# Opening of a hybrid decoder block on one core: small constants loaded behind the norm of x, large transfers first, identity transposes ahead of the first turns, TensorE too in written order

## The chip, the cores and the metric

One core of one Trainium2 chip runs the whole program. The metric is the device time of one launch in microseconds (us), lower is better. The core has TensorE (PE; its weight loads are the rows PEld), VectorE (DVE), ScalarE (ACT), GpSimd (POOL) and SyncE (SP, which here only issues DMAs; ACT issues some too).

## The reference

A decoder block on x of 1 x 1024 x 1024 in float32. What matters here is its beginning:

```
u = rms_norm(h, mix_pre_g)                        # x * rsqrt(mean(x*x) + eps) * g
z = einsum('bsd,de->bse', u, w_in)                # d = 1024, e = 512 + 3*512 + 2*1024
p, q, k, v = z[..., :o1], z[..., o1:o2], z[..., o2:o3], z[..., o3:o4]
lam = exp(sum(lam_q1*lam_k1)) - exp(sum(lam_q2*lam_k2)) + lambda_init
```

Then follow a pooling mixer (p, scaled by pool_scale), differential attention on four heads (q, k, v, lam, gain subln_g), two sigmoid gates, an output projection and a SwiGLU network of width 2816.

## The kernel before, in words

Every float32 matrix is split in two float32r parts, hi (a cast, on ACT) and lo = value - hi (a subtraction, on DVE or POOL), and a product is three matmuls: hi*hi, lo*hi, hi*lo (`mac`, L105 to L107; `triple`, L230 to L232).

The opening works on eight blocks of 128 tokens, `tb` 0 to 7. For each, SP loads 128 x 1024 of x (`load_x`, L302). ACT squares and sums it (`square`, L127), DVE makes the mean (`ms`, L122), POOL the power -0.5 (`rstd`, L123), DVE multiplies x by it and by the gain `g1` (`normed`, L348). PE turns the block with eight 128 x 128 transposes against an identity (`x_t`, L379; I call this a turn) into one of two PSUM buffers of the tag "pair". From there ACT casts `A_hi` (L383), DVE subtracts `A_lo` (L86), and ACT copies a plain float32 version (`A_raw` for blocks 0 to 3, L399; `S_raw` for 4 to 7, L402), from which DVE builds the sums S1 to S4 that the later units need (L159). Meanwhile the q and k weights of heads 0 and 1 come in as four tiles of 1024 x 128 (`w_raw`, L205), cast by ACT (`w_hi`, L327) and split by POOL (`w_lo`, L332, in four pieces).

As soon as two blocks are turned, `first_pair` multiplies them for head 0: q and k, 24 matmuls of 256 columns each (a half pair is one of the two). There are four pairs. Then come head 1's q and k, 4 times 24 matmuls of 512 columns (`common(1, ...)`), and then fourteen units of the projection. A unit (`seven`, L250 to L280) is seven products of 12 matmuls of 512 columns with operands A11, S1, S2, A12, S3, S4, A22 and weight sums made by `weights` (`Wh`, `Wl`, `wf_t`). Results of heads 0 to 3 go through `qk_done` (ACT L310 or L163, DVE L311 or L86, a store by ACT, L314) to DRAM.

The scheduler of the language sets the order on an engine, except inside `tc.manual_schedule` (L358), where the named engines keep the written order; before, these are ACT, DVE and POOL, and PE is left to the scheduler. Six small constants (`psc`, `sgc`, four lambda vectors into a tile `sg`; L430 to L434) are written behind the opening but no data holds them back, and the scheduler puts their DMAs first on ACT.

Every DMA of SP and ACT signals one of eight counters, and a DMA that takes up a counter again first waits for its earlier transfer.

Of the kernel before, what the change touches and what calls it, by code (L numbers as in the profile page):

```python
# [31 lines left out]
A8, B4 = 16, 14  # L32
QORDER = (7, 0, 6, 1, 5, 2, 4, 3)
LAG = 4
PACES = (2.2, 0.5, 0.3, 0.3)


@with_exitstack
def block_kernel(ctx, tc, x, w_in, pool_mix, pool_scale, w_branch_a, lam_q1, lam_k1, lam_q2,
# [42 lines left out]
    def f32(ap):  # L82
        return ap.bitcast(F32)
# [221 lines left out]
    def qk_done(h, e, t, src, st=None):  # L305
# [44 lines left out]
    for tb in range(2):  # L350
        xts.append(load_x(tb))
    nc.sync.dma_start(g1, mix_pre_g.partition_broadcast(P))
    xts.append(load_x(2))
    first_raw(0)
    first_raw(1)
    for tb in range(3, 5):
        xts.append(load_x(tb))
    with tc.manual_schedule(engines={nc.scalar.engine, nc.vector.engine, nc.gpsimd.engine}):  # L358
        for tb in range(2):
            square(tb)  # L360
            rstd(tb)
        for tb in range(2):
            normed(tb)
# [5 lines left out]
        o = [(fil("q"), fil("k")), (mm("q"), mm("k"))]

        def first_pair(i):
            for e in range(2):
                common(0, e, i // 2, o[i // 2][e], slice(i % 2 * 2 * P, (i % 2 + 1) * 2 * P))

        for tb in range(NB):
            t, cols = tb // 4, slice(tb % 4 * P, (tb % 4 + 1) * P)
            both = pair("x_t")
            for k in range(KD):
                nc.tensor.transpose(both[:, k // 4, k % 4 * P:(k % 4 + 1) * P], xts[tb][:, k * P:(k + 1) * P], ident)  # L379
            v = [both[:, kq, :].rearrange("p (k t) -> p k t", k=4) for kq in range(2)]  # L380
            ops = [[a[:, :, cols] for a in U[f"A{t + 1}{kq + 1}"]] for kq in range(2)]
            for kq in range(2):
                nc.scalar.copy(ops[kq][0], v[kq])  # L383
            if tb + 3 < NB:
                square(tb + 3)
            if tb in (0, 2, 4):
                first_hi(tb // 2 + 1)
            for kq in range(2):
                sub(ops[kq][1], v[kq], ops[kq][0])
            if tb + 2 < NB:  # L390
                normed(tb + 2)
            if tb + 3 < NB:
                rstd(tb + 3)
            if tb < 6:
                for part in range(2):
                    first_lo(tb // 2 + 1, part + tb % 2 * 2)
            if t == 0:
                for kq in range(2):
                    nc.scalar.copy(traws[f"A1{kq + 1}"][:, :, cols], v[kq])  # L399
            else:  # L400
                s1, s2, s3, s4 = (traws[f"S{i + 1}"][:, :, cols] for i in range(4))
                nc.scalar.copy(s1, v[0])  # L402
                tt(s1, v[1], s1, ALU.add)
                tt(s2, s1, s2, ALU.subtract)
                tt(s3, v[1], s2, ALU.subtract)
                tt(s4, s4, s2, ALU.subtract)
            if tb + 5 < NB:
                xts.append(load_x(tb + 5))
            if tb < 2:
                first_raw(tb + 2)  # L410
            if tb in (3, 5, 7):
                first_pair(tb // 2 - 1)
            if tb == 7:
                for e in range(2):
                    qk_done(0, e, 0, o[0][e])
    first_pair(3)
    for e in range(2):
        qk_done(0, e, 1, o[1][e])
    W = weights(w_cols(o_q, 2), w_cols(o_k, 2))
    for t in range(2):  # L420
        o = (fil("q"), fil("k")) if t == 0 else (mm("q"), mm("k"))
        for e in range(2):
            common(1, e, t, o[e], slice(0, HALF))
            qk_done(1, e, t, o[e])
    for n in ("S1", "S2", "S3", "S4"):
        U[n] = operand(n)
        split(U[n], traws[n])
# [4 lines left out]
    lamt = temp("sg").rearrange("p (i d) -> p i d", d=HD)
    for i, t in enumerate(lams):
        nc.scalar.dma_start(lamt[:, i, :], t.partition_broadcast(P))  # L434
    lsum, lexp, nlam = small(2, "lsum"), small(2, "lexp"), cp.tile([P, 1], F32, name="nlam")
    for i in range(2):
        nc.vector.tensor_tensor_reduce(out=lamt[:, 4, :], in0=lamt[:, 2 * i, :], in1=lamt[:, 2 * i + 1, :],
                                       scale=1.0, scalar=0.0, op0=ALU.mult, op1=ALU.add,
                                       accum_out=lsum[:, i:i + 1])
    nc.scalar.activation(lexp, lsum, AF.Exp)  # L440

    nc.vector.tensor_tensor(out=nlam, in0=lexp[:, 1:2], in1=lexp[:, 0:1], op=ALU.subtract)
    nc.vector.tensor_scalar(nlam, nlam, -LAMBDA_INIT, None, op0=ALU.add)
    nc.scalar.mul(sgc, sgc, 1.0 - LAMBDA_INIT)
    for g, w in enumerate(WINDOWS):
        nc.gpsimd.iota(cnt[:, g, :], pattern=[[1, 16]], base=1, channel_multiplier=0,
                       allow_small_or_imprecise_dtypes=True)
        nc.vector.tensor_scalar(cnt[:, g, :], cnt[:, g, :], float(w), None, op0=ALU.min)
# [692 lines left out]
```

## Time and profile before

| what | value |
|---|---|
| median of 3 runs | 1298.51 us (1295.7 to 1298.53) |
| the profiled execution, its own time | 1296.83 us |
| its span, first to last instruction | 1295.0 us |
| PE busy, of the span | 1250.5 us (97%) |
| DVE, ACT, POOL busy | 837.8, 581.2, 139.5 us |
| mean granted TensorE clock | 0.997 |

The profile shows the profiled execution alone; its own time is 1.83 us above its span, which lies around the first and last instruction. A busy PE is not PE at its peak, since matmuls overlap and their ends are modelled; the spacing of starts is the better measure of pace. PE is idle nearly only at the ends of the span: the first of forty slices is 40% busy, the second 80%, the last 70%, the others 90% or more apart from two at 80%.

### The profile page before, as it was taken

The page shows a single profiled execution, that of the slowest core. Times are in us where ns is not written, and L with a number is a line of the kernel's source. Part 1 is how long each engine was busy: PE and PEld are TensorE (multiplying, and loading weights), DVE is VectorE, ACT ScalarE, POOL GpSimd, SP SyncE. Part 2 cuts the span into 40 slices and gives each one's busy share as a digit, 9 for nine tenths or more (in the row PEclk, how much of TensorE's full clock was granted, in tenths as well). Part 3 has the DMA queues.
Part 4 walks back from the last instruction along what each step waited for, and adds up shares of the span by engine and source line. Part 5 has one row for each costly group of instructions (what it writes and reads, how often), then busy time and mean ns, then how long its engine had stood idle before and what let it go on. Part 6 is the DMA issues. An engine that isn't in the chain of part 4 may idle for free.

```text
span 1295.0 us, 15657 instructions
## 1 busy us (share of the span) xinstructions
PE 1250.5 (97%) x5856; PEld 1036.0 (80%) x5856; DVE 837.8 (65%) x1301; ACT 581.2 (45%) x1033; POOL 139.5 (11%) x128
## 2 busy tenths in 40 slices
PE   4899999999989998999999999999999999999997
PEld 4788778888778887878878888888888888888886
DVE  4875676444369997655499565565565538965666
ACT  6443335344486675144464333333333334444542
POOL 3100000000101010001102101111110111000221
PEclk9999999999999999999999999999999999999999
DMA  7254346332598411543333232333223258732235
GB/s 247 67 179 161 104 148 207 120 130 103 166 284 220 143 54 57 160 165 131 113 107 109 93 101 99 104 122 119 85 90 114 98 195 291 256 104 90 90 106 203
DMA packets 139788, 179.16 MB, mean 138 GB/s; under 512 B 8000, under 2 KB 94528, under 8 KB 137280
## 3 DMA queue, kind: packets, MB, share of 16 engines
q1 hardware_dynamic: 127776, 146.56, 35.7%
q10 hardware_dynamic: 11936, 31.60, 6.4%
q8 instruction: 46, 0.75, 0.2%
q14 instruction: 30, 0.25, 0.1%
HBM read 124.39 MB, written 53.74 MB: 138 GB/s over the span
## 4 chain that ended last, share of the span: by engine, by line
PE 81%; DVE 7%; DMA 4%; ACT 4%; issue 2%; POOL 1%; ACTq 0%; DVEq 0%; SPq 0%; POOLq 0%
PE Y L230 10%; PE Y L231 10%; PE Y L232 9%; PE X L230 5%; PE X L232 5%; PE X L231 5%; PE Yd L231 3%; PE Yd L232 3%; PE Yd L230 2%; PE Z L231 2%; PE Z L232 2%; PE Z L230 2%; PE o L653 2%; PE wo L794 2%; PE wo L795 2%
## 5 line engine op out<-in xcount | busy, mean ns | idle before, releaser
L159 DVE TENSOR_TENSOR p<-Z,p 128x512 f32<-128x512 f32 x35 | 24.2, 691 | 158.8 <-PE Z L232 158.8
L231 PE MATMUL Y<-A_lo,Wh 128*128 128x512 f32 x296 | 115.7, 391 | 0.3 <-DVE A_lo L86 0.3
L230 PE MATMUL Y<-A_hi,Wh 128*128 128x512 f32 x296 | 115.3, 390 | 0.0
L232 PE MATMUL Y<-A_hi,Wl 128*128 128x512 f32 x296 | 115.2, 389 | 0.0
L230 PE MATMUL X<-S_hi,Wh 128*128 128x512 f32 x280 | 109.1, 390 | 0.1
L231 PE MATMUL Y<-S_lo,Wh 128*128 128x512 f32 x280 | 109.2, 390 | 0.0
L230 PE MATMUL Y<-S_hi,Wh 128*128 128x512 f32 x280 | 109.1, 390 | 0.0
L232 PE MATMUL Y<-S_hi,Wl 128*128 128x512 f32 x280 | 109.1, 390 | 0.0
L232 PE MATMUL X<-S_hi,Wl 128*128 128x512 f32 x280 | 109.0, 389 | 0.0
L231 PE MATMUL X<-S_lo,Wh 128*128 128x512 f32 x280 | 109.0, 389 | 0.0
L199 ACT CAST Wh<-wf_t 128x1024 fp32r<-128x1024 f32 x70 | 72.6, 1050 | 70.3 <-PE X L231 30.8
L86 DVE TENSOR_TENSOR w_op<-wd,w_op 128x512 fp32r<-128x512 f32 x77 | 56.3, 731 | 53.6 <-ACT w_op L163 53.5
L86 DVE TENSOR_TENSOR Wl<-wf_t,Wh 128x1024 fp32r<-128x1024 f32 x70 | 86.6, 1245 | 4.7 <-ACT Wh L199 4.7
L199 ACT CAST Wh<-w_raw 128x1024 fp32r<-128x1024 f32 x72 | 60.4, 841 | 63.1 <-PE Z L231 41.9
L163 ACT CAST w_op<-wd 128x512 fp32r<-128x512 f32 x77 | 47.9, 622 | 80.7 <-PE Yd L232 32.5
L86 DVE TENSOR_TENSOR Wl<-w_raw,Wh 128x1024 fp32r<-128x1024 f32 x72 | 69.6, 967 | 14.4 <-ACT Wh L199 14.4
L231 PE MATMUL Yd<-w_op,s_op 128*128 128x512 f32 x176 | 68.7, 390 | 0.3 <-DVE w_op L86 0.2
L230 PE MATMUL Yd<-w_op,s_op 128*128 128x512 f32 x176 | 68.6, 390 | 0.0
L232 PE MATMUL Yd<-w_op,s_op 128*128 128x512 f32 x176 | 68.3, 389 | 0.0
L159 DVE TENSOR_TENSOR wf_t<-w_raw,wf_t 128x512 f32<-128x512 f32 x70 | 65.8, 940 | 1.0
L231 PEld LDWEIGHTS Y<-A_lo,Wh 128*128 128x128 f32 x296 | 55.6, 188 | 12.0 <-DVE A_lo L86 0.7
L230 PEld LDWEIGHTS Y<-A_hi,Wh 128*128 128x128 f32 x296 | 55.6, 188 | 11.5
(259 smaller groups left out, 3050.6 us busy)
## 6 DMA issues: line engine op xcount, KB each, us to landing
s_raw<-fsd SPq DMA_DIRECT2D x35, 512.0 KB, 3.5
w_raw<-in_w_in_dram SPq DMA_DIRECT2D x32, 512.0 KB, 3.9
w_raw<-in_w_ffn_gate_dram SPq DMA_DIRECT2D x22, 512.0 KB, 3.6
w_raw<-in_w_ffn_up_dram SPq DMA_DIRECT2D x22, 512.0 KB, 3.6
fsd<-fss SPq DMA_DIRECT2D x11, 1024.0 KB, 3.9
wd<-in_w_ffn_down_dram SPq DMA_DIRECT2D x44, 256.0 KB, 5.3
fsd<-F SPq DMA_DIRECT2D x33, 256.0 KB, 2.2
qkd<-qk_st ACTq DMA_DIRECT2D x16, 512.0 KB, 3.6
```

The lines of the kernel that those rows point to most:

```text
L86: nc.vector.tensor_tensor(out=o, in0=a, in1=f32(hi), op=ALU.subtract)
L159: nc.vector.tensor_tensor(out=o, in0=a, in1=b, op=op)
L163: nc.scalar.copy(hi, a)
L199: nc.scalar.copy(hi, a)
L230: nc.tensor.matmul(o, ah, bh, start=start, stop=False, skip_group_check=goes_on)
L231: nc.tensor.matmul(o, ah, bl, start=False, stop=False, skip_group_check=goes_on)
L232: nc.tensor.matmul(o, al, bh, start=False, stop=stop, skip_group_check=goes_on)
L653: nc.tensor.matmul(o, ats[b // 4][:, j, b % 4 * P:(b % 4 + 1) * P], V[:, b, :, :], start=b == 0 and j == 0, stop=b == qb and j == 1)
L794: nc.tensor.matmul(o[e], mh[:, k, :], wl, start=False, stop=False)
L795: nc.tensor.matmul(o[e], ml[:, k, :], wh, start=False, stop=k == KD - 1)
```

## The change

It touches the opening alone. PE joins the engines in written order. x, the gain and the weights are loaded in another order; the six constants are loaded by SP, behind the first weights of the units, into tiles that POOL clears first. PE begins with 40 transposes of the identity by itself, and repeats eight transposes of a block behind the first two turns, into a PSUM bank (`k_157`) that is not yet in use. The half pairs are dealt out between the turns. The plain copies and the sums are made in other pieces. The `qk_done` stores stand behind the big splits. The pool `wp` is allocated ahead of `sm`, and `g1` sits in `wp`.

```diff
+WARM = 40
     sb = ctx.enter_context(tc.tile_pool(name="sb", bufs=2))
+    wp = ctx.enter_context(tc.tile_pool(name="wp", bufs=2))
     sm = ctx.enter_context(tc.tile_pool(name="sm", bufs=4))
...
-    g1 = b4([P, D], F32, "g1")
+    g1 = wp.tile([P, D], F32, tag="wlo", bufs=2, name=name("g1"))
...
+    xts.append(load_x(0))
+    nc.sync.dma_start(g1, mix_pre_g.partition_broadcast(P))
+    xts.append(load_x(1))
+    first_raw(0)
+    xts.append(load_x(2))
+    first_raw(1)
+    for tb in range(3, 6):
         xts.append(load_x(tb))
+    first_raw(2)
...
+            nc.tensor.transpose(o[1][1][:, i % 4 * P:(i % 4 + 1) * P], src[:, k:k + P], ident)
...
+    with tc.manual_schedule(engines={nc.tensor.engine, nc.scalar.engine, nc.vector.engine, nc.gpsimd.engine}):
+        warm(WARM)
+        square(0)
+        rstd(0)
+        normed(0)
+        turn(0)
+        warm(KD, xts[0])
...
+        turn(1)
+        warm(KD, xts[1])
...
+        for tb in range(2, NB):
+            if tb == 2:
+                first_pair(0, 0)
+            turn(tb)
+            if tb > 2:
+                first_pair((tb - 2) // 2, (tb - 2) % 2)
+            turned_hi(tb)
+            if tb + 1 < NB:
+                normed(tb + 1)
+            turned_lo(tb)
+            if tb + 2 < NB:
+                square(tb + 2)
+                rstd(tb + 2)
+            turned_raw(tb)
...
+            if tb in (3, 5):
                 first_hi(tb // 2 + 1)
+                for part in range(4):
+                    first_lo(tb // 2 + 1, part)
+        for t in (psc, sgc, lamt):
+            nc.gpsimd.memset(t, 0.0)
...
+        half_sums(6, 8, "S1", "S2")
+        U["S1"] = operand("S1")
+        split(U["S1"], traws["S1"])
+        store()
...
-    nc.scalar.dma_start(psc, pool_scale.rearrange("(g p) -> p g", p=P))
-    nc.scalar.dma_start(sgc, subln_g.rearrange("(p o) -> p o", o=1))
...
+    nc.sync.dma_start(psc, pool_scale.rearrange("(g p) -> p g", p=P))
+    nc.sync.dma_start(sgc, subln_g.rearrange("(p o) -> p o", o=1))
+    for i, t in enumerate(lams):
+        nc.sync.dma_start(lamt[:, i, :], t.partition_broadcast(P))
```

How the order moves, at three places. Line numbers of the changed kernel are its own. First SP at the very start, with what each DMA waits for (DMAHW0 to 7 are the eight counters). Before:

```order
L302 DMA xt_128<-in_x_dram 128x1024
L302 DMA xt_130<-in_x_dram 128x1024
L352 DMA g_13_95<-in_mix_pre_g_dram 128x1024 [waits DMAHW0_49]
L302 DMA xt_133<-in_x_dram 128x1024 [waits DMAHW1_49]
L205 DMA w_raw_135<-in_w_in_dram 128x8x128 [waits DMAHW2_49]
L205 DMA w_raw_139<-in_w_in_dram 128x8x128 [waits DMAHW3_49]
L302 DMA xt_143<-in_x_dram 128x1024 [waits DMAHW4_49]
```

Now:

```order
L303 DMA xt_128<-in_x_dram 128x1024
L355 DMA g_13_95<-in_mix_pre_g_dram 128x1024
L303 DMA xt_131<-in_x_dram 128x1024
L206 DMA w_raw_133<-in_w_in_dram 128x8x128
L303 DMA xt_137<-in_x_dram 128x1024
L206 DMA w_raw_139<-in_w_in_dram 128x8x128
L303 DMA xt_143<-in_x_dram 128x1024
L303 DMA xt_145<-in_x_dram 128x1024
L303 DMA xt_147<-in_x_dram 128x1024 [waits DMAHW0_49]
```

Before, the six constants on ACT's queue hold six of the eight counters, so the third DMA of SP waits for one of them; now eight large transfers go out without a wait.

Second, PE from its first instruction. Before, three blocks are turned ahead of the first product (q of blocks 0 and 1):

```order
L379 MATMUL x_t_178<-ident,xt_128 128x128 x8
L379 MATMUL x_t_209<-ident,xt_130 128x128 x8
L379 MATMUL x_t_239<-ident,xt_133 128x128 x8
L105 MATMUL q_174<-A_hi_83,w_hi_137 128x256
L106 MATMUL q_174<-A_lo_84,w_hi_137 128x256
```

Now the identity is transposed 40 times first, two turns are each repeated, and the first half pair stands ahead of the third turn:

```order
L370 MATMUL k_157<-ident 128x128 x40
L380 MATMUL x_t_207<-ident,xt_128 128x128 x8
L370 MATMUL k_157<-ident,xt_128 128x128 x8
L380 MATMUL x_t_238<-ident,xt_131 128x128 x8
L370 MATMUL k_157<-ident,xt_131 128x128 x8
L106 MATMUL q_154<-A_hi_83,w_hi_135 128x256
L107 MATMUL q_154<-A_lo_84,w_hi_135 128x256
```

Third, ACT where block 7 is copied. Before, `sgc`'s scaling is ACT's first computation (the row `L444 ACTIVATE sgc<-sgc`); now it stands between the casts and the plain copies of block 7, and waits for its DMA:

```order
L387 CAST A_hi_87<-x_t_529 128x4x128 [waits PE_49]
L387 CAST A_hi_89<-x_t_529 128x4x128
L600 ACTIVATE sgc<-sgc 128x1 [waits DMAHW2_49]
L396 COPY S_raw_93<-x_t_529 128x4x128 [waits DVE_49]
L396 COPY S_raw_94<-x_t_529 128x4x128
L311 ACTIVATE qk_st_575<-q_154 128x512
```

On DVE the first product of the lambda vectors moves in the same way, to a place ahead of three of the sums and of the first `qk_st` (q of head 0, bank `q_154`):

```order
L160 TENSOR_TENSOR S_raw_93<-S_raw_93,S_raw_94 128x4x128
L593 ISA sg_153,lsum_1054<-sg_153 128x64 [waits DMAHW4_49,DMAHW3_49,Pool_49]
L593 ISA lsum_1054 128x1
L160 TENSOR_TENSOR A_raw_91<-S_raw_93,A_raw_91 128x4x128 [waits DVE_49]
L160 TENSOR_TENSOR S_raw_94<-S_raw_94,A_raw_91 128x4x128 [waits DVE_49]
L160 TENSOR_TENSOR A_raw_92<-A_raw_92,A_raw_91 128x4x128
L312 SCALAR_TENSOR_TENSOR qk_st_575<-q_154,qk_st_575 128x512 [waits Activation_49]
```

Behind the first unit of the projection the order of PE, DVE, ACT and POOL is the same as before.

## Rows read from the trace of the kernel before

**Rows 1.** The page's first two parts: busy time of each engine over the span, and PE's busy share in forty equal slices (tenths).

```profile
PE 1250.5 (97%) x5856; PEld 1036.0 (80%) x5856; DVE 837.8 (65%) x1301; ACT 581.2 (45%) x1033; POOL 139.5 (11%) x128
PE   4899999999989998999999999999999999999997
```

**Rows 2.** Busy time by stretch: the stretch in us, its length, then busy us and instructions of PE, PEld, DVE, ACT and POOL, granted clock, DMA share, GB/s.

```profile
0.00:12.60 12.60, 0.00 (x0) 0.00 (x0) 2.61 (x10) 3.67 (x6) 2.18 (x12) 1.00 0.71 216
16.30:20.38 4.08, 0.00 (x1) 0.01 (x1) 2.64 (x4) 3.78 (x8) 2.62 (x6) 1.00 1.05 323
37.80:40.74 2.94, 0.00 (x0) 0.03 (x1) 2.94 (x5) 0.00 (x0) 1.04 (x1) 1.00 0.10 23
40.74:44.50 3.76, 3.76 (x20) 3.71 (x21) 3.76 (x6) 1.57 (x3) 0.00 (x0) 0.57 0.41 124
44.50:50.44 5.94, 5.74 (x46) 5.33 (x44) 5.63 (x13) 1.73 (x4) 0.00 (x0) 0.98 0.00 0
50.44:52.52 2.08, 0.00 (x1) 0.00 (x0) 2.03 (x6) 0.04 (x1) 0.00 (x0) 1.00 0.00 0
58.13:79.90 21.77, 21.77 (x98) 18.03 (x97) 17.95 (x18) 10.24 (x13) 0.00 (x0) 1.00 0.65 215
79.90:140.80 60.90, 60.90 (x273) 50.18 (x272) 35.42 (x50) 23.38 (x34) 0.00 (x0) 1.00 0.41 132
```

**Rows 3.** What PE waited for in the first 300 us: total us, times, longest.

```profile
PE x_t L379 <- DVE xt L348: 12.6, 1, 12.6
PE x_t L379 <- ACT A_raw L399: 4.1, 1, 4.1
PE x_t L379 <- DVE S_raw L159: 2.9, 1, 2.9
PE y L105 <- ACT yh L163: 1.0, 2, 0.7
```

**Rows 4.** PE in order of time: start, us, what. 256-column matmuls early and later, a turn early (two, x16) and later (x8), the first 512-column matmul.

```profile
12.64 3.65 PE L379 MATMUL x_t<-ident,xt 128*128 128x128 f32 x16 [12.64 <-DVE xt L348]
22.57 0.41 PE L107 MATMUL q<-A_hi,w_lo 128*128 128x256 f32 x1
22.79 0.41 PE L105 MATMUL q<-A_hi,w_hi 128*128 128x256 f32 x1
...
29.68 1.04 PE L379 MATMUL x_t<-ident,xt 128*128 128x128 f32 x8
...
34.52 0.28 PE L105 MATMUL k<-A_hi,w_hi 128*128 128x256 f32 x1
34.64 0.28 PE L106 MATMUL k<-A_lo,w_hi 128*128 128x256 f32 x1
...
58.13 0.40 PE L105 MATMUL q<-A_hi,w_hi 128*128 128x512 f32 x1
```

**Rows 5.** SP's DMA queue: its wait for `psc` (total us, times, longest), and its first two issues (start, us for both).

```profile
SPq L352 <- DMA psc<-in_pool_scale_dram: 4.0, 1, 4.0
...
0.74 0.86 SPq L302 DMA_DIRECT2D xt<-in_x_dram  x2
```

**Rows 6.** DMA issues with the us from issue to landing: x's first block (issued at 0.74), the gain, one weight load alone at 33.6, then (min/median/max) the lambda loads and all loads of x; and all engines' stretch of 8 to 24 us (last figure GB/s).

```profile
xt<-in_x_dram SPq DMA_DIRECT2D x1, 512.0 KB, 4.0
g<-in_mix_pre_g_dram SPq DMA_DIRECT2D x1, 512.0 KB, 5.6
w_raw<-in_w_in_dram SPq DMA_DIRECT2D x1, 512.0 KB, 3.8
sgc<-in_subln_g_dram ACTq DMA_DIRECT2D x1, 0.5 KB, 5.8
DMA to landing us min/median/max: 4.8/5.2/5.5
DMA to landing us min/median/max: 4.0/6.0/9.0
8.00:24.00 16.00, 7.27 (x33) 6.90 (x34) 8.97 (x18) 10.94 (x21) 6.66 (x14) 1.00 1.05 338
```

**Rows 7.** Groups by line and shape in the first 82 us: busy us, mean ns of one, idle before.

```profile
L127 ACT ACTIVATE junk<-xt 128x1024 bf16<-128x1024 f32 x8 | 8.5, 1066 | 0.5 <-DMA xt<-in_x_dram 0.5
L123 POOL TENSOR_TENSOR rstd<-ms,mhalf 128x1 f32<-128x1 f32 x8 | 4.4, 553 | 17.1 <-DVE ms L122 9.8 <-DVE cnt L448 7.2
L348 DVE SCALAR_TENSOR_TENSOR xt<-xt,rstd,g 128x1024 f32<-128x1024 f32 x8 | 10.1, 1278 | 1.1 <-DMA g<-in_mix_pre_g_dram 1.0
L332 POOL TENSOR_TENSOR w_lo<-w_raw,w_hi 128x256 fp32r<-128x256 f32 x16 | 11.8, 762 | 4.2 <-ACT w_hi L327 4.2
```

**Rows 8.** ACT and DVE in order of time, where work is back to back: start, us, what.

```profile
32.20 1.09 ACT L127 ACTIVATE junk<-xt 128x1024 bf16<-128x1024 f32 x1
33.25 1.07 ACT L327 CAST w_hi<-w_raw 128x1024 fp32r<-128x1024 f32 x1
34.67 1.12 ACT L383 CAST A_hi<-x_t 128x512 fp32r<-128x512 f32 x2
...
56.38 0.68 DVE L311 SCALAR_TENSOR_TENSOR qk_st<-q,qk_st 128x512 fp32r<-128x512 f32 x1
56.98 2.28 DVE L86 TENSOR_TENSOR S_lo<-S_raw,S_hi 128x2048 fp32r<-128x2048 f32 x1
59.18 2.29 DVE L86 TENSOR_TENSOR S_lo<-A_raw,S_hi 128x2048 fp32r<-128x2048 f32 x1
```

More of the change, by code (lines that the diff above doesn't have):

```diff
@@ L55, in block_kernel @@
     dr = ctx.enter_context(tc.tile_pool(name="dr", bufs=1, space=bass.MemoryType.DRAM))
-    wp = ctx.enter_context(tc.tile_pool(name="wp", bufs=2))
     uid = [0]
@@ L303, in load_x, with qk_done @@
         return xt
-    def qk_done(h, e, t, src, st=None):
+    def qk_done(h, e, t, src, st=None, stores=None):
         st = b4([P, 2, HALF], F32R, "qk_st") if st is None else st[e][:, :, half(t)]
@@ L313, in qk_done @@
             split((hi, lo), src)
-        nc.scalar.dma_start(qkd[h][e][:, :, half(t)], f32(st))
+        if stores is None:
+            nc.scalar.dma_start(qkd[h][e][:, :, half(t)], f32(st))
+        else:
+            stores.append((qkd[h][e][:, :, half(t)], f32(st)))
     firsts = [(h, e) for h in range(2) for e in range(2)]
@@ L348, in normed @@
         nc.vector.scalar_tensor_tensor(out=xts[tb], in0=xts[tb], scalar=xr[tb], in1=g1, op0=ALU.mult, op1=ALU.mult)
-    for tb in range(2):
-        xts.append(load_x(tb))
[L352 to L363, printed above, removed]
-        first_hi(0)
-        for part in range(4):
-            first_lo(0, part)
+    xts.append(load_x(0))
@@ new lines, in block_kernel, with warm @@
+    nc.sync.dma_start(g1, mix_pre_g.partition_broadcast(P))
[4 more added lines that the diff above has]
+    for tb in range(3, 6):
+        xts.append(load_x(tb))
+    first_raw(2)
+    lamt = temp("sg").rearrange("p (i d) -> p i d", d=HD)
+    o = [(fil("q"), fil("k")), (mm("q"), mm("k"))]
+    def warm(n, src=ident):
+        for i in range(n):
+            k = i % (src.shape[-1] // P) * P
+            nc.tensor.transpose(o[1][1][:, i % 4 * P:(i % 4 + 1) * P], src[:, k:k + P], ident)
@@ new lines, in block_kernel, with first_pair, turn @@
+    views = {}
+    def first_pair(i, e):
+        common(0, e, i // 2, o[i // 2][e], slice(i % 2 * 2 * P, (i % 2 + 1) * 2 * P))
+    def turn(tb):
+        both = pair("x_t")
+        for k in range(KD):
+            nc.tensor.transpose(both[:, k // 4, k % 4 * P:(k % 4 + 1) * P], xts[tb][:, k * P:(k + 1) * P], ident)
+        cols = slice(tb % 4 * P, (tb % 4 + 1) * P)
+        views[tb] = cols, [(both[:, kq, :].rearrange("p (k t) -> p k t", k=4),
+                            [a[:, :, cols] for a in U[f"A{tb // 4 + 1}{kq + 1}"]]) for kq in range(2)]
@@ new lines, in turned_hi, with turned_lo, turned_raw, half_sums @@
+    def turned_hi(tb):
+        for v, (hi, lo) in views[tb][1]:
+            nc.scalar.copy(hi, v)
+    def turned_lo(tb):
+        for v, (hi, lo) in views[tb][1]:
+            sub(lo, v, hi)
+    def turned_raw(tb):
+        cols, ((v0, _), (v1, _)) = views[tb]
+        for n, v in zip(("A11", "A12") if tb < 4 else ("S1", "S3"), (v0, v1)):
+            nc.scalar.copy(traws[n][:, :, cols], v)
+    def half_sums(b0, b1, *names):
+        cols = slice((b0 - 4) * P, (b1 - 4) * P)
+        a22, s1, s2, s4 = (traws[n][:, :, cols] for n in ("S3", "S1", "S2", "S4"))
+        for n in names:
+            if n == "S1":
+                tt(s1, s1, a22, ALU.add)
+            elif n == "S2":
+                tt(s2, s1, s2, ALU.subtract)
+            elif n == "S3":
+                tt(a22, a22, s2, ALU.subtract)
+            else:
+                tt(s4, s4, s2, ALU.subtract)
@@ new lines, in block_kernel @@
+    with tc.manual_schedule(engines={nc.tensor.engine, nc.scalar.engine, nc.vector.engine, nc.gpsimd.engine}):
[5 more added lines that the diff above has]
+        warm(KD, xts[0])
+        square(1)
+        rstd(1)
+        normed(1)
+        turned_hi(0)
+        first_hi(0)
+        first_lo(0, 0)
+        first_lo(0, 1)
+        turned_lo(0)
+        turn(1)
+        warm(KD, xts[1])
+        xts.append(load_x(6))
+        first_raw(3)
+        xts.append(load_x(7))
+        turned_hi(1)
+        first_lo(0, 2)
+        first_lo(0, 3)
+        turned_lo(1)
@@ L367, in block_kernel @@
         square(2)
         rstd(2)
[L369 to L386, printed above, removed]
-                first_hi(tb // 2 + 1)
[L388 to L415, printed above, removed]
@@ L416, in block_kernel @@
-    first_pair(3)
-    for e in range(2):
[L418 to L427, printed above, removed]
-    nc.scalar.dma_start(psc, pool_scale.rearrange("(g p) -> p g", p=P))
@@ L431, in block_kernel @@
-    nc.scalar.dma_start(sgc, subln_g.rearrange("(p o) -> p o", o=1))
[L432 to L448, printed above, removed]
@@ L449, in block_kernel @@
-    nc.vector.reciprocal(cnt, cnt)
+        normed(2)
+        first_hi(1)
+        first_lo(1, 0)
+        square(3)
+        rstd(3)
+        for part in range(1, 4):
+            first_lo(1, part)
+        turned_raw(0)
+        turned_raw(1)
+        for tb in range(2, NB):
[12 more added lines that the diff above has]
+            turned_raw(tb)
+            if tb == 5:
+                half_sums(4, 5, "S1", "S2")
+            if tb == 6:
+                half_sums(4, 5, "S3", "S4")
+            if tb == 7:
+                half_sums(5, 6, "S1", "S2", "S3", "S4")
+            if tb in (3, 5):
+                first_hi(tb // 2 + 1)
+                for part in range(4):
+                    first_lo(tb // 2 + 1, part)
@@ new lines, in block_kernel, with store @@
+        for t in (psc, sgc, lamt):
+            nc.gpsimd.memset(t, 0.0)
+        stores = []
+        def store():
+            while stores:
+                nc.scalar.dma_start(*stores.pop(0))
+        for e in range(2):
+            qk_done(0, e, 0, o[0][e], stores=stores)
+        first_pair(3, 0)
+        first_pair(3, 1)
+        half_sums(6, 8, "S1", "S2")
+        U["S1"] = operand("S1")
+        split(U["S1"], traws["S1"])
+        store()
+        for e in range(2):
+            qk_done(0, e, 1, o[1][e], stores=stores)
@@ new lines, in block_kernel @@
+        U["S2"] = operand("S2")
+        split(U["S2"], traws["S2"])
+        store()
+        W = weights(w_cols(o_q, 2), w_cols(o_k, 2))
+        half_sums(6, 8, "S3", "S4")
+        U["S3"] = operand("S3")
+        split(U["S3"], traws["S3"])
+        o = fil("q"), fil("k")
+        for e in range(2):
+            common(1, e, 0, o[e], slice(0, HALF))
+            qk_done(1, e, 0, o[e], stores=stores)
+        U["S4"] = operand("S4")
+        split(U["S4"], traws["S4"])
+        store()
+        o = mm("q"), mm("k")
@@ L451, in block_kernel @@
+        for e in range(2):
+            common(1, e, 1, o[e], slice(0, HALF))
+    for e in range(2):
+        qk_done(1, e, 1, o[e])
     later = []
@@ L527, in block_kernel @@
              W=W if h == 2 else None, done=partial(qk_done, h, st=[a8([P, 2, S], F32R, "qk_st") for _ in range(2)]))
+    nc.sync.dma_start(psc, pool_scale.rearrange("(g p) -> p g", p=P))
+    nc.sync.dma_start(sgc, subln_g.rearrange("(p o) -> p o", o=1))
+    for i, t in enumerate(lams):
+        nc.sync.dma_start(lamt[:, i, :], t.partition_broadcast(P))
+    lsum, lexp, nlam = small(2, "lsum"), small(2, "lexp"), cp.tile([P, 1], F32, name="nlam")
+    for i in range(2):
+        nc.vector.tensor_tensor_reduce(out=lamt[:, 4, :], in0=lamt[:, 2 * i, :], in1=lamt[:, 2 * i + 1, :],
+                                       scale=1.0, scalar=0.0, op0=ALU.mult, op1=ALU.add,
+                                       accum_out=lsum[:, i:i + 1])
+    nc.scalar.activation(lexp, lsum, AF.Exp)
+    nc.vector.tensor_tensor(out=nlam, in0=lexp[:, 1:2], in1=lexp[:, 0:1], op=ALU.subtract)
+    nc.vector.tensor_scalar(nlam, nlam, -LAMBDA_INIT, None, op0=ALU.add)
+    nc.scalar.mul(sgc, sgc, 1.0 - LAMBDA_INIT)
+    for g, w in enumerate(WINDOWS):
+        nc.gpsimd.iota(cnt[:, g, :], pattern=[[1, 16]], base=1, channel_multiplier=0,
+                       allow_small_or_imprecise_dtypes=True)
+        nc.vector.tensor_scalar(cnt[:, g, :], cnt[:, g, :], float(w), None, op0=ALU.min)
+    nc.vector.reciprocal(cnt, cnt)
     for h in reversed(range(NH)):
```

## The prediction

> **What bounds the kernel now.** I read the page's totals first, then busy time by stretch, then PE's waits, then PE's rows in order of time. PE is busy 97% of the span and only its first two slices stand out [rows 1]. By stretch: PE does nothing until 12.6 us, is idle again for 4.1, 2.9 and 2.1 us, and from 58.13 us on it never stops until 140.8: 21.77 of 21.77 and 60.90 of 60.90 us [rows 2]. The first wait behind that is for data of the program's own chain (PE `y` for ACT `yh`) [rows 3]. So the end moves with the moment at which the unbroken run begins, and what the opening loses ahead of 58.13 is all that can be won. Its work on PE is eight turns and eight half pairs of 24 matmuls. At the full clock a matmul of 256 columns starts 0.12 us after the last and a turn costs about 0.9 (1.04 with its tail), so 8 x 24 x 0.12 + 8 x 0.9 = 30.2 us; it takes 45.5, from 12.6 to 58.1. [...]
>
> **The start (counters and order of loads).** SP could not issue the gain until the DMA of `psc` had landed, 4.0 us [rows 5]. Now eight large transfers go out unhindered. x's first block lands 4.0 us after its issue at 0.74 [rows 5, 6], at 4.7. With the queue full, 338 GB/s flow [rows 6], so each further 512 KB takes 1.55 us: gain 6.3, second block 7.8, weights 9.4, third block 10.9, second weights 12.5, fourth block 14.0. Upper end: loads of x took up to 9.0 us to land [rows 6], and I allow 1.5 us more at the start of the chain.
>
> Chain to the first product: block 1 at 7.8, square and its read-out 1.25, mean 0.15, power 0.55, `normed` 1.28 [rows 7] gives 11.0; its turn ends at 11.9. ACT casts the two halves by 12.9 (1.0 for two with the tail [rows 8]); DVE's lo ends at 14.2. The weights' cast follows block 0's, 9.8 to 10.8, and POOL's four pieces at 0.75 [rows 7] end at 13.8. The half pair therefore starts at about 13 and ends at about 17 instead of starting at 22.0.
>
> Next, turns 2 and 3. Both PSUM buffers of the turns are in use until ACT has made the plain copies, which the change puts behind square 2, cast `w_hi` and square 3: 12.9 + 1.05 + 0.95 + 1.05 + 0.95 = 16.9 for block 0 and 17.9 for block 1 (a square 1.05, a cast or two copies 0.95 [rows 8]). So turn 2 runs 17.0 to 17.9, and turn 3 waits for `normed` of block 3 until about 19. From there PE has five turns and seven half pairs, 5 x 0.9 + 7 x 2.88 = 24.7 us. Per block ACT needs a pair of casts, a square and a pair of copies, 3.0 us, against PE's 3.8, so ACT keeps up except where it also casts 1024 weights (0.95, twice). I add 1.0 us for such waits. The pairs end at 19.0 + 24.7 + 1.0 = **44.7**, against 58.1: a gain of 13.4.
>
> The 56 extra transposes cost nothing if they end before `normed` of block 0 at 7.9 and block 1 at 11.0. The identity is ready near 1.4 us. At the low level a transpose took 0.228 us (sixteen in 3.65), so if the clock rises during the forty as it did in later bursts of about 3.7 us [rows 2, 4], they end near 8. In the trace no burst of transposes alone lasted past 3.65 us, so it doesn't show whether they raise the clock. I take it that they do; the other case is the first rival.
>
> **The price: constants behind weights.** ACT's `sgc` and DVE's first lambda product now stand ahead of work for block 7 and of the first `qk_st`, whose reading frees the bank into which PE's first 512-column product (head 1) writes. Their DMAs stand on SP behind a weight load that waits for POOL's last `w_lo`. ACT reaches the fourth `w_hi` after 4 casts, 4 squares, 4 copies and one weight cast from 17.9, 12.8 us plus some 3 of waits for PE's pace: that cast is done at 34.6, POOL done 37.5. SP issues the weights, `psc`, `sgc` (38.5) and the lambdas (two out by 39.4) at about 0.45 each. Landings took 3.8 us (a load alone), 4.8 to 5.5 (lambdas) and 5.8 (`sgc`) [rows 6]: `sgc` between 42.3 and 44.3, the lambda pair between 43.2 and 44.9. DVE then does the product (0.3), three sums (1.8) and `qk_st` (0.6), which sets PE's start at 45.9 to 47.6; ACT's copies and `qk_st` end no later. Against 44.7 that is 1.2 to 2.9 us. I take 1.6, nearer to the lone load because only one 512 KB transfer lies ahead. Bounds: 0, and 6.3 if they land as late as x's slowest, 9.0 us.
>
> **DVE behind it.** From there to the `qk_st` that frees the bank of head 1's second q, DVE's row holds 15 operations of 512 columns (0.60 apart), 7 of 1024 (1.15, an estimate between its neighbours), 4 of 2048 (2.20) [rows 8] and 0.4 of small ones: 26.3, plus about 2.1 waiting for ACT's casts, 28.4 us. PE has four products of 5.44 us (a quarter of the 21.77 [rows 2]) and two products of the unit, 2.72 each, 27.2 us. PE waits 1.2; I take 1.3, bounds 0 and 3.
>
> The rest is free: clearing three small tiles on POOL has no reader waiting but those DMAs, the allocation of pools changes addresses alone, the later stores on ACT have a reader hundreds of matmuls on.
>
> **Sum.** 13.4 - 1.6 - 1.3 = 10.5 us. From the profiled execution's 1296.83 that is 1286.3. The runs shown lie from 1.1 below it to 1.7 above (the median); I add 1.2 and forecast **1287.5 us**. Bounds of the terms: gain from 13.4 (no wait) to 13.4 - 1.5 - 6.3 - 1.3 = 4.3.
>
> **Rivals.**
> 1. Transposes do not raise the clock. Then forty last 9.1 us, to 10.5, each turn and repeat 1.8, and the first half pair begins at 17.7, at 0.22 per matmul at first. Turn 3 begins near 22.6 instead of 19.0, the pairs end at 48.3, which hides the constants; 58.1 - 48.3 - 1.3 leaves 8.5, less about 1 for the slow start: 7.5, or 1290.5. For it: the sixteen transposes of [rows 4] all ran at the low level. Against: they were cut off by idleness. Chance 0.17. [...]
> 2. Constants land like the slowest x. ACT and DVE stand until 48, PE's head 1 starts near 51: gain 13.4 - 6.3 - 1.3 = 5.8, or 1292. For it: `sgc` took longest of the small ones, and it is now queued behind 512 KB. Against: little else is in flight at 38 us. Chance 0.14.
> 3. Slower: the low clock through the whole opening. PE in written order waits ahead of each turn; if those waits reach the 2.94 us behind which the clock had fallen, instead of the 2.08 behind which it held [rows 2], each half pair costs 24 x 0.22 = 5.3 and each turn 1.8. From 13: 8 x 5.3 + 6 x 1.8 = 53.2, to 66.2, 8 us later than now: 1306. It decides once about six tenths of the matmuls run at the low level. Against: my waits are 0.1 to 0.8 us. Chance 0.04.
> 4. No change. Something behind the opening holds its own time and takes the gain back. Against: PE never stops from 58 to 140.8, and then waits for its own chain. Chance 0.07: about 1297.
> 5. More: landings early enough that neither wait appears, 13.4 us: 1284. Chance 0.05.
>
> **How the numbers follow.** My forecast has the remaining 0.53, with a range of its own of 1284.5 to 1290. A measurement can tell about 0.3% of this kernel, 3.9 us, from no change. Faster by more: forecast, rivals 1 and 5, and nearly all of 2, 0.87. Within: rival 4 and an edge of 2, 0.08. Slower: rival 3 and a little for what I overlooked, 0.05. The range takes in rivals 1, 2 and 5 and leaves out 3 and most of 4: 1282.5 to 1294.5.
>
> **What would show it.** In the profile after: SP issues eight loads in the first 4.5 us; the first half pair starts near 13 with matmuls 0.12 apart (0.22: rival 1); the first 512-column matmul stands at 45 to 48 us; just ahead of it ACT waits for `sgc` and DVE for a lambda DMA; PE has one or two waits of about 1 us for DVE near 70; from there all rows keep their distances. I am wrong if the pairs end past 50, if the two DMA waits exceed 5 us, or if PE's later rows have shifted by another amount than the 512-column matmuls have.

## The result, and the profile after

The change takes 1286.41 us (median; 1285.56 to 1287.64) against 1296.92 (1295.7 to 1298.53): a ratio of 0.9915, 95% interval 0.9905 to 0.9925. The forecast was 1287.5. The spans of the profiled executions are 1283.9 and 1295.0 us, 11.1 apart. So the number was right; this section and the next show that its parts were not. Some of the opening's gain did not come, and about as much came from a stage 500 us behind it.

The page's totals and slices, which answer to [rows 1]: the first slice has risen from 4 tenths to 8.

```profile
PE 1254.4 (98%) x5912; PEld 1041.6 (81%) x5912; DVE 835.6 (65%) x1297; ACT 583.3 (45%) x1037; POOL 142.7 (11%) x131
PE   8899999999989998999999999999999999999997
PEclk9899999999999999999999999999999999999999
```

PE in order of time (start, us, what, and in brackets the idle time before and what ended it), which answers to [rows 4]:

```profile
1.42 7.25 PE L370 MATMUL k<-ident 128*128 128x128 f32 x40 [1.42 <-POOL ident masks.py:199]
8.50 1.04 PE L380 MATMUL x_t<-ident,xt 128*128 128x128 f32 x8
11.40 1.09 PE L380 MATMUL x_t<-ident,xt 128*128 128x128 f32 x8 [0.98 <-DVE xt L352]
14.38 0.38 PE L107 MATMUL q<-A_lo,w_hi 128*128 128x256 f32 x1 [0.83 <-DVE A_lo L87]
17.65 1.09 PE L380 MATMUL x_t<-ident,xt 128*128 128x128 f32 x8 [0.26 <-ACT A_raw L396]
20.11 1.06 PE L380 MATMUL x_t<-ident,xt 128*128 128x128 f32 x8 [1.37 <-DVE xt L352]
...
45.41 0.28 PE L108 MATMUL k<-A_hi,w_lo 128*128 128x256 f32 x1
48.97 0.80 PE L106 MATMUL q<-A_hi,w_hi 128*128 128x512 f32 x1 [3.27 <-DVE qk_st L312]
49.56 0.63 PE L107 MATMUL q<-A_lo,w_hi 128*128 128x512 f32 x1
...
54.68 0.42 PE L107 MATMUL q<-A_lo,w_hi 128*128 128x512 f32 x1
...
57.23 0.39 PE L106 MATMUL k<-A_hi,w_hi 128*128 128x512 f32 x1
```

Read it from the top. The forty transposes end at 8.7, and the first turn already takes 1.04 us, as the later turn in [rows 4] does. Turn 3 is the last turn to wait for its operand, at 20.11, and the pairs end at 45.5. Then PE stands for 3.27 us at head 1, and from there to 54.68 the 512-column matmuls start 0.43 us apart. Busy time by stretch (columns as in [rows 2]) has the granted clock beside that:

```profile
48.97:54.68 5.71, 5.71 (x14) 4.51 (x14) 4.97 (x6) 3.95 (x4) 0.00 (x0) 0.50 0.47 174
54.68:57.23 2.55, 2.55 (x13) 2.09 (x11) 2.55 (x4) 1.13 (x2) 0.00 (x0) 1.00 0.26 96
```

Thirteen matmuls start behind the wait at a granted clock of 0.50 (the row counts the next one too, which starts at the window's end); the product of 24 takes 8.26 us (48.97 to 57.23) where one at 1.00 takes 5.44, a quarter of the 21.77 in [rows 2].

What held PE back, on ACT, DVE and SP's queue (same columns as the PE rows; the first row is SP's seventh to ninth load, for the account below):

```profile
4.21 4.86 SPq L303 DMA_DIRECT2D xt<-in_x_dram  x3
...
39.36 0.50 SPq L588 DMA_DIRECT2D sgc<-in_subln_g_dram  x1
...
40.38 0.43 SPq L590 DMA_DIRECT2D sg<-in_lam_k_dram  x1
43.04 0.20 ACT L600 ACTIVATE sgc<-sgc 128x1 f32<-128x1 f32 x1 [4.02 <-DMA sgc<-in_subln_g_dram]
45.78 0.22 DVE L593 CUSTOM_DVE_ANT_0 sg<-sg 128x64 f32<-128x64 f32 x1 [4.84 <-DMA sg<-in_lam_k_dram]
48.23 0.68 DVE L312 SCALAR_TENSOR_TENSOR qk_st<-q,qk_st 128x512 fp32r<-128x512 f32 x1
```

**Where the gain lies.** To find it, take the same instructions in both traces. A tile's rows give count, min/median/max ns of one, and the first and last start. First before, then the change:

```profile
L105 PE MATMUL y<-yh,pm x8: 389/389/504, 147.6 to 211.8; 128*128 128x512 f32 x8
L731 PE MATMUL oT<-ident,O x32: 270/272/329, 503.0 to 512.5; 128*128 128x128 f32 x32
L793 PE MATMUL wo<-woh,mh x128: 390/393/501, 554.1 to 652.8; 128*128 128x512 f32 x128
```

```profile
L106 PE MATMUL y<-yh,pm x8: 389/391/501, 141.3 to 205.5; 128*128 128x512 f32 x8
L810 PE MATMUL oT<-ident,O x32: 270/272/330, 495.8 to 505.2; 128*128 128x128 f32 x32
L872 PE MATMUL wo<-woh,mh x128: 388/389/497, 545.9 to 641.5; 128*128 128x512 f32 x128
```

The first 512-column matmul stands 9.2 us earlier (48.97 for 58.13), the first `y` 6.3, the first `oT` 7.2, the last `wo` 11.3. So 4.1 us came between `oT` and `wo`, where the code has not changed: in the branch product with `w_branch_b` and the `wo` product. The median duration in the `wo` row is the hint: 393 ns before, 389 now. Over 20 us inside the branch product (columns as in [rows 2]; before, then the change) PE is busy throughout at a granted clock of 1.00 in both, yet does 88 matmuls in one and 90 in the other:

```profile
516.00:536.00 20.00, 20.00 (x88) 16.21 (x87) 12.65 (x20) 1.86 (x3) 0.00 (x0) 1.00 0.50 157
```

```profile
516.00:536.00 20.00, 20.00 (x90) 16.57 (x89) 12.03 (x19) 3.20 (x5) 0.00 (x0) 1.00 0.51 160
```

From one start to the next the mean is 0.2324 us (branch) and 0.2326 (`wo`) before, and 0.2272 and 0.2274 now (176 and 362 gaps, leaving out those of 0.3 us and more); the unit products show 0.2268 to 0.2270 in both kernels. The expectations below call the fast spacing 0.2267. In these two stages the stationary operand (`wb_hi`, `wb_lo`, `mh`, `ml`) lies in the weight pool and the moving one in the pool `sb`; in the unit products both lie in `sb`. The other branch product has the same split, but is spread through attention.

### The profile page after: what moved, and what is told of

Read it like the earlier page. It is cut to its first block, busy times and chain, and to the rows that moved or that the text cites. A ratio compares the mean times of both kernels' runs of the same rounds, so it can differ in the third digit from the quotient of the medians.

```text
span 1283.9 us, 15774 instructions
## 1 busy us (share of the span) xinstructions
PE 1254.4 (98%) x5912; PEld 1041.6 (81%) x5912; DVE 835.6 (65%) x1297; ACT 583.3 (45%) x1037; POOL 142.7 (11%) x131
## 4 chain that ended last, share of the span: by engine, by line
PE 81%; DVE 7%; DMA 4%; ACT 3%; issue 2%; POOL 2%; SPq 0%; ACTq 0%; DVEq 0%; POOLq 0%
PE Y L231 9%; PE Y L232 9%; PE Y L233 9%; PE X L231 5%; PE X L232 5%; PE X L233 5%; PE Yd L232 3%; PE Yd L233 3%; PE Yd L231 3%; PE Z L232 2%; PE Z L233 2%; PE Z L231 2%; PE o L732 2%; PE wo L873 2%; PE wo L874 2%
```

## The experiments

Ratios are to the kernel before, run on the same chip.

**The pools back.** Edit, of the changed kernel:

```
+    sm = ctx.enter_context(tc.tile_pool(name="sm", bufs=4))
     wp = ctx.enter_context(tc.tile_pool(name="wp", bufs=2))
-    sm = ctx.enter_context(tc.tile_pool(name="sm", bufs=4))
```

> The changed kernel with the weight pool behind the small pool again, nothing else. In its profile the 384 matmuls of the two branch products that read wb_hi and wb_lo and the 384 of wo that read mh and ml stand 0.2267 us apart on average, in the profile of before 0.2324; their stationary operands lie in the weight pool, whose addresses this line moves (in before 128x4-byte rows from byte 201472 on, 256 above a multiple of 512; in the change from 192640 on, 128 above one). Theory A: the addresses cost before 768 x 0.0057 = 4.4 us, so this kernel takes about 1290.5 us and its branch matmuls are 0.232 apart. Theory B: the 4.8 us that the change won behind its opening came from other timing (transfers, waits): 1286.4 us and 0.2267.

Measured: 1289.7 us, 0.9938 (0.9923 to 0.9953). The slow spacing is back:

```profile
516.00:536.00 20.00, 20.00 (x87) 16.20 (x86) 11.40 (x18) 3.43 (x5) 0.00 (x0) 1.00 0.45 145
L872 PE MATMUL wo<-woh,mh x128: 388/393/497, 545.3 to 643.6; 128*128 128x512 f32 x128
```

The order of all instructions is the same as in the change, and the mean spacing is 0.2325 and 0.2326 us, so A holds: addresses alone do it. It is the spacing that shows it; by time alone the interval meets the change's (0.9905 to 0.9925).

**The pools alone.** In the kernel before, the weight pool is allocated ahead of the small pool, as in the change, and nothing else.

> The kernel before with the order of the two pools alone changed. Theory A (addresses of stationary operands): 1296.9 - 4.4 = 1292.5 us, branch and wo matmuls 0.2267 apart, rows ahead of 350 us where they were. Theory B (other timing): 1296.9 us, 0.2324.

Measured: 1296.23 us, 0.9991 (0.9981 to 1.0001): the time alone decides nothing. In its profile the branch and `wo` matmuls are 0.2271 and 0.2275 apart and from the first `oT` to the last `wo` it takes 147.7 us against 149.8 before; but its opening was 2.0 us later in that execution (first `y` at 149.6). The gain is there in its place, and is less than the 4.4 expected.

**The address, not the place.** Four kernels differ from the change only in where the pools begin. Addresses are bytes, as the programs allocate them. Edits: the pools back and 96 unused floats in the small pool; 32 in the weight pool; 32 and 96 in the first pool, ahead of all others, as in

```
+    cp.tile([P, 32], F32, tag="pad", bufs=1, name="pad")
```

> The weight pool behind the small pool again, but with 384 unused bytes in the small pool, so that the weight pool starts at byte 201856, 128 above a multiple of 512 as in the change, 9 KB further up than there. Theory A: what counts is the address modulo 512 (or a divisor of it): the branch and wo matmuls stand 0.2267 us apart as in the change. Theory B: what counts is how far up the pool lies: 0.2324 as with the pools back.

> The changed kernel, weight pool ahead of the small pool, with 128 unused bytes at its start, so that its tiles begin 256 above a multiple of 512 as in before, at about the change's place. Theory A (the address modulo 512 decides, not the place): branch and wo matmuls stand 0.2324 us apart, about 3 us more: 1290. Theory B (the place): 0.2267 and 1287.

> The changed kernel with all pools moved up by 128 bytes: operands of all products, stationary and moving, begin 256 above a multiple of 512. Theory A (a stationary operand at 256 is read slower, whatever the moving one): the X, Y, Z and Yd matmuls too stand 0.2324 apart, some 4,000 x 0.0057 = 23 us more: 1310. Theory B (the two operands' addresses must agree modulo 512): 0.2267 everywhere, 1287.

> The changed kernel with all pools moved up by 384 bytes, so that all operands begin at a multiple of 512. Theory A (some residues of a stationary operand are slow): 0.2267 or 0.2324 everywhere, so 1287 or 1310; below 0.2267 only if the residue 128 is a slow one too. Theory B (agreement): 0.2267 everywhere, 1287.

The same stretch in each, in this order:

```profile
516.00:536.00 20.00, 20.00 (x90) 16.57 (x89) 11.61 (x18) 3.44 (x5) 0.00 (x0) 1.00 0.46 149
```

```profile
516.00:536.00 20.00, 20.00 (x88) 16.08 (x87) 11.78 (x19) 2.48 (x4) 0.00 (x0) 1.00 0.45 142
```

```profile
516.00:536.00 20.00, 20.00 (x90) 16.57 (x89) 11.36 (x18) 2.41 (x4) 0.00 (x0) 1.00 0.54 168
```

```profile
516.00:536.00 20.00, 20.00 (x90) 16.57 (x89) 11.80 (x18) 2.17 (x4) 0.00 (x0) 1.00 0.52 163
```

| kernel | stationary mod 512 | moving mod 512 | matmuls in 20 us | first `oT` to first `wo`, us | first `oT` to last `wo`, us |
|---|---|---|---|---|---|
| before | 256 | 128 | 88 | 51.0 | 149.8 |
| pools back | 256 | 128 | 87 | 51.0 | 149.3 |
| weight pool up 128 | 256 | 128 | 88 | 51.2 | 148.7 |
| the change | 128 | 128 | 90 | 50.1 | 145.7 |
| pools back, padded | 128 | 128 | 90 | 50.1 | 148.4 |
| pools alone | 128 | 128 | 89 | 50.1 | 147.7 |
| all up 128 | 256 | 256 | 90 | 50.1 | 146.5 |
| all up 384 | 0 | 0 | 90 | 50.1 | 146.9 |

Place is out (third to fifth rows), and so is a bad residue as such: with all operands at 256 nothing is slow. What is slow in these kernels is a stationary and a moving operand whose addresses differ by 128 modulo 512: 87 or 88 matmuls in the 20 us, against 89 or 90. Theory A of the first two kernels and theory B of the last two hold. The way from the first `oT` to the first `wo` sorts all fourteen profiled executions of this document: 51.0 to 51.2 us in the four with disagreeing addresses, 50.1 in the ten others. The modulus itself is not shown: 256 would sort these kernels in the same way. One time each: 1287.91, 1291.11, 1287.17 and 1287.70 us. The padded kernel's 148.4 is not spacing: its clock fell to 0.72 for 6 us behind waits at the start of `wo`.

**The change once more.**

> The changed kernel itself once more, beside the others on one chip: a ratio near 0.9915 to the kernel before, and a second profile. Theory A: stages behind the opening last as long in every execution, so the wo stage takes again 95.6 us from its first to its last matmul. Theory B: that stage's waits for w_out and its splits vary between executions (98.1 us in the run with the filler, 97.6 with the pools alone): it differs by 1 us or more here, with the opening the same within 0.5.

Measured: 1287.03 us, 0.9924 (0.9911 to 0.9938). First `y` at 139.9 instead of 141.3, last `wo` at 643.0 instead of 641.5; from `oT` to `wo` 146.6 us. Both theories miss: `wo` itself takes 96.5 instead of 95.6, within 1, but the opening is not the same within 0.5. Its wait at head 1 is 3.1 us, and behind it seven matmuls start 0.42 to 0.43 us ahead of the next where the first execution had twelve (granted clock 0.61 from 48.5 to 52.0): that product took 7.18 us instead of 8.26.

**Constants issued early.** The six loads stand behind the last load of x, without the cleared tiles.

> The changed kernel with the six small loads issued right behind the last load of x instead of behind three cleared tiles, so that they have landed by about 30 us. Theory A: the wait for them sets PE's start of head 1; without it the 3.3 us of waiting and the 2.6 us that the low clock behind it cost go: 1286.4 - 5.9 = 1280.5 us, or 1281.8 if DVE then holds PE up by 1.3 near 70 us. Theory B: DVE's or ACT's own work ends about as late, so that PE waits nearly as long: 1286.4.

Measured: 1285.27 us, 0.9907 (0.9892 to 0.9922), not clear of the change. The edit tested less than it should: with the loads early, the scheduler put ACT's scaling of `sgc` early too, into the middle of the turns, where ACT waited 2.8 us for it. Head 1 starts at 48.07, with matmuls 0.23 us apart from the first, right behind pairs that now end there instead of at 45.5. So A's wait is gone and has come back as late pairs.

**Filler.**

```
         first_pair(3, 1)
+        hold = pair("hold")
+        for i in range(28):
+            nc.tensor.transpose(hold[:, 0, i % 4 * P:(i % 4 + 1) * P], ident, ident)
```

> The changed kernel with 28 transposes of the identity into a free bank between the last half pair and head 1's first product, where PE stands idle for 3.3 us: 28 x 0.11 = 3.1 us of work that nobody reads. Theory A: the idleness lets the clock fall; with the filler the 512-column matmuls are 0.227 apart from the first, against 0.427 for the first 5.5 us: 2.6 us less, 1283.8. Theory B: something else slows these matmuls, or the filler pushes them back by as much: 1286.4 or more.

Measured: 1286.35 us, 0.9916 (0.9901 to 0.9931): no gain in time. Yet the clock held, 25 matmuls in 5.5 us at 1.00, and then a wait appeared that the change does not have (by stretch, then PE's waits: total us, times, longest):

```profile
48.50:54.00 5.50, 5.46 (x25) 4.48 (x25) 4.75 (x7) 3.65 (x4) 0.00 (x0) 1.00 0.44 165
PE Y L231 <- DVE qk_st L312: 0.4, 1, 0.4
```

The product ahead of that wait takes 3.40 us from start to start and the one before it 3.01, instead of 2.72: PE has run into DVE's row, about 1.0 us. The first `y` stands at 139.4, 1.9 and 0.5 earlier than in the two executions of the change, and the stages behind gave that back in this execution (148.2 us from `oT` to `wo`). From head 1 to the first `y` it takes 90.8 us, 1.3 more than the 89.5 of before. A is right on the clock and wrong on the price.

**Constants pinned.** Loads early as above, and what reads them at the end of the written order:

```
             common(1, e, 1, o[e], slice(0, HALF))
+        lsum, lexp, nlam = small(2, "lsum"), ...
+        ...
+        nc.scalar.mul(sgc, sgc, 1.0 - LAMBDA_INIT)
```

> The changed kernel with the six small loads right behind the last load of x, and with what reads them (the lambda products, their exponential, the scaling of sgc) behind head 1's products in the written order instead of ahead of the first qk_st. Theory A: PE's 3.3 us of waiting at head 1 and the low clock behind it (2.6 us) go: head 1 starts at 46 instead of 48.97, the first y matmul stands at 135.5 to 137 instead of 141.3, and the time is 1280.5 us, up to 1282 if DVE holds PE up near 70. Theory B: the stages behind give the gain back (waits in the wo stage grow by as much as the opening wins): 1285 to 1286.4.

Measured: 1282.56 us, 0.9890 (0.9877 to 0.9904), against 1287.03 for the change on the same chip. Head 1 follows the last pair without a gap, at a granted clock of 1.00 from 45.0 to 48.5:

```profile
45.10 0.28 PE L108 MATMUL k<-A_hi,w_lo 128*128 128x256 f32 x1
45.22 0.40 PE L106 MATMUL q<-A_hi,w_hi 128*128 128x512 f32 x1
45.46 0.40 PE L107 MATMUL q<-A_lo,w_hi 128*128 128x512 f32 x1
```

The first `y` is at 134.8, 5.1 and 6.5 earlier than in the change, and most of it reaches the end. A holds to within 0.6 us of its upper figure for the time, and the first `y` came earlier still than its 135.5 to 137. This version beats both kernels.

**The same with the pools back.**

> The kernel with the constants pinned (0.9890 of the kernel before) with the weight pool behind the small pool again: the same instructions in the same order on every engine, only the weight pool's addresses differ (256 above a multiple of 512 instead of 128, while the moving operands lie 128 above one). Theory A (disagreeing addresses): branch and wo matmuls 0.2324 apart instead of 0.2267, about 3.2 us between the first oT and the last wo matmul: 1285.8 us, a ratio near 0.9915, with the first y matmul where it was (134.8 within 0.5). Theory B (addresses cost nothing in time, since that stretch waits for w_out anyway): 1282.6, 0.9890.

Measured: 1284.78 us, 0.9904 (0.9888 to 0.9921). The intervals overlap, so the time alone does not tell A from B. The profile does: first `y` at 134.9, 88 matmuls in the 20 us, and 149.7 us from `oT` to `wo` against 147.3.

```profile
516.00:536.00 20.00, 20.00 (x88) 16.24 (x87) 12.45 (x19) 2.82 (x4) 0.00 (x0) 1.00 0.51 163
```

**Without the extra transposes.**

```
-        warm(WARM)
-        warm(KD, xts[0])
-        warm(KD, xts[1])
```

> The changed kernel without the forty transposes of the identity and without the two repeated turns, which nobody reads. Theory A: they raise the clock before the first turn. Without them the two first turns and part of the first half pair run at 0.22 per 256-column matmul; about 2.5 us later at the half pair's end, of which the waits ahead of turns 2 and 3 (0.26 and 1.37 us) hide 1.6: 1287 us, up to 1288.5. Theory B: they change nothing, since the clock rises with the first products anyway and PE waits later: 1286.4 us.

Measured: 1288.99 us, 0.9940 (0.9926 to 0.9954), 2.0 above the change on the same chip. The intervals overlap a little, but all five times lie above all four of the change, and head 1 starts at 50.47 where the seven executions with the change's order of work start it at 48.2 to 49.1. A holds, a little above its upper figure. The first two turns take 1.97 us each where they took 1.04 and 1.09 in the change, and the matmuls of the first half pair start 0.21 to 0.22 apart from the third on, not 0.12:

```profile
7.87 1.97 PE L380 MATMUL x_t<-ident,xt 128*128 128x128 f32 x8 [7.87 <-DVE xt L352]
11.43 1.97 PE L380 MATMUL x_t<-ident,xt 128*128 128x128 f32 x8 [1.60 <-DVE xt L352]
```

## Why the prediction was right, and where it was not

**The start: right.** SP issues the first six loads by 3.41 and no longer waits for `psc`. The eight by 4.5 that I named did not come: the seventh issue lasts from 4.21 to 8.12 and the eighth starts at 8.16. Nothing waited for it; ACT waits for x only with the first two blocks. The first product starts at 13.2 (forecast 13), turn 2 at 17.65 (17.0), turn 3 at 20.11 (19), and the pairs end at 45.5 instead of 44.7. The 12.6 us from 58.1 to 45.5 are the main term, sized to 0.8. Turn 3 is late because `normed` of blocks 2 and 3 took 1.84 and 1.74 us where I had 1.28, with POOL's `w_lo` running beside both; whether that is the reason no run tests.

```profile
15.65 1.84 DVE L352 SCALAR_TENSOR_TENSOR xt<-xt,rstd,g 128x1024 f32<-128x1024 f32 x1 [0.66 <-POOL rstd L124]
18.22 1.74 DVE L352 SCALAR_TENSOR_TENSOR xt<-xt,rstd,g 128x1024 f32<-128x1024 f32 x1 [0.67 <-POOL rstd L124]
```

**The warm-up: right, and rival 1 is out.** Forty transposes took 7.25 us, 6.25 when the change ran again, not the 9.1 of 0.228 us each (the forecast's low level); nothing else ran on PE, and the turn behind them takes 1.04 us. So the pace rose during them. The granted clock does not show it: it reads 1.00 from 1.42 to 8.50. Taking the transposes out cost 2.0 us.

**Price 1: right mechanism, half its size.** PE waits 3.27 us (3.1 again) where I took 1.6. DVE's lambda product decided it, ACT being done earlier. Its load was issued about 1 us later than I had it, and it landed as slowly as before's lambdas, not like the lone load that I chose: the product starts 5.4 us after the issue, and [rows 6] had 4.8 to 5.5 for just these loads. I set aside the row of the same transfer for one that looked similar.

**What the wait does to the clock: left out.** This is the larger miss in the opening. [Rows 2] showed a low clock behind 2.94 us of idleness, and I let the wait range up to 6.3 us without pricing that. It cost 8.26 - 5.44 = 2.8 us (1.7 again). Eight of the profiled executions waited at head 1, for 2.1 to 3.5 us. Against the 89.5 us from head 1 to the first `y` of the pinned kernel, which did not wait, six of them took 1.7 us more, and two took 2.8 and 2.9. The length of the wait does not sort them: 2.9 stands behind 3.1 us, 1.7 behind 2.5 and behind 3.5.

**Price 2: right, but covered.** The 1.3 us for DVE did not appear, because the low clock kept PE back by more. With the clock held by filler it came out at about 1.0 by the two products, and 1.3 on the way from head 1 to the first `y`. In the change DVE goes from the end of the first `qk_st` at 48.9 to the end of the one that frees the bank at 77.2, 28.3 us for the 28.4 forecast. The clock's cost and DVE's are alternatives here: PE pays the larger. The sum's lower bound of 4.3 us put 1.3 here and not the 3 that I named as this term's bound; with 3 it is 2.6.

**"The allocation of pools changes addresses alone": the step that failed.** I costed it at nothing. It is worth some 2 to 3 us: by spacing 576 x 0.0053 = 3.1, and from `oT` to `wo` the four profiled executions with disagreeing addresses took 148.7 to 149.8 us, mean 149.4, the ten with agreeing ones 145.7 to 148.4, mean 147.1. That it is less by this way than by spacing fits waits at the start of `wo`, which vary between executions: `wo` takes 95.6 and 96.5 us in the two of the change. No pair of whole times shows it clear of noise: with the pools in either order the intervals overlap, in the change and in the pinned kernel, and the interval of the pools alone reaches 1.

So the opening gave 6.3 us in the profiled execution (7.7 again) and not 10.5; the addresses and lucky waits at the start of `wo` (4.1 us together, 3.2 again) and 0.9 ahead of `oT` (a loss of 1.1 again) made up the sum. That they did is luck. My own sign of being wrong, PE's later rows shifting by another amount than the 512-column matmuls, is what showed it. Rivals 2 and 3 did not come: the wait was half of rival 2's, and ahead of turns the longest wait was 1.4 us (1.5 again).

What stays open: why disagreeing addresses slow these matmuls, whether a difference other than 128 does, and what makes the low clock last 5.7 us in one execution and less in the next.

## What to carry to other kernels

When a wait on PE is priced, price also slow matmuls behind it (here 2.8 us behind a wait of 3.27), and ask which later wait they cover. Here removing one of two such terms brought out the other (a ratio of 0.9916 with filler, 0.9915 without), and only removing both, by moving the readers of late constants and not the loads alone, paid (0.9890). Compare the start times of the same instructions at several places along the kernel, not the totals: a forecast that matches at the end can be two errors of opposite sign. Do not cost a change of allocation at nothing until the spacing of back-to-back matmuls is seen to be the same (here 0.2324 us before, 0.2272 after).

## What the runs showed of the hardware

- Back-to-back fp32 matmuls of 512 columns in the branch product start 0.2324 to 0.2333 us apart on average where the stationary operand's byte address and the moving one's differ by 128 modulo 512 (four kernels), and 0.2267 to 0.2272 where they agree, at 0, 128 or 256 (nine executions of eight kernels; in the tenth, without the extra transposes, the 50.1 us from the first `oT` to the first `wo` show it). The granted clock reads 1.00 in the stretches shown above of both. So the spacing depends on the two addresses together in these runs; no run shows by what mechanism.
- Forty transposes with nothing else on PE took 6.06 to 7.25 us, and the turn behind them 1.04 to 1.09. Without them the first two turns took 1.97 us each.
- In these runs the length of a single wait does not sort whether the clock falls. At the start of `wo` PE waits 1.21 us in the padded kernel and in the pinned one; behind it the clock fell in the first (0.72 over 6 us) and held in the second (1.00). At head 1 it fell behind 2.13 us without the extra transposes (0.77 over 7.53 us), where in the kernel before it held at 1.00 behind 2.08 [rows 2]. The rows are of the padded kernel, the pinned one, the one without extra transposes, and the kernel before:

```profile
551.41 0.79 PE L874 MATMUL wo<-wol,mh 128*128 128x512 f32 x1 [1.21 <-DVE wol L88]
551.41:557.41 6.00, 6.00 (x19) 4.85 (x20) 2.97 (x4) 1.35 (x2) 0.00 (x0) 0.72 0.56 175
```

```profile
546.22 0.50 PE L871 MATMUL wo<-wol,mh 128*128 128x512 f32 x1 [1.21 <-DVE wol L87]
546.22:552.22 6.00, 5.74 (x24) 4.44 (x25) 3.01 (x4) 1.21 (x2) 0.00 (x0) 1.00 0.53 175
```

```profile
50.47 0.50 PE L106 MATMUL q<-A_hi,w_hi 128*128 128x512 f32 x1 [2.13 <-DVE qk_st L312]
50.47:58.00 7.53, 7.53 (x26) 6.04 (x27) 6.79 (x9) 4.69 (x4) 0.00 (x0) 0.77 0.37 139
```

```profile
52.52:54.52 2.00, 2.00 (x16) 2.00 (x17) 1.37 (x4) 1.16 (x3) 0.00 (x0) 1.00 0.03 8
```
